# Summing three modulation sections by rows on DVE instead of TensorE, and splitting part of the weights by DMA, in an RG-LRU and retention trunk

## Chip, cores and metric

One NeuronCore of one Trainium2 chip. Times are device microseconds (us) of one execution. The kernel before was run three times; the changed kernel is compared by its median.

## What is computed

Two layers act on 512 latent tokens and 256 context tokens (768 in all) of width 1024. Cut to what matters here:

```python
def modulation(cond, mod_w, mod_b):            # cond: (1024,), mod_w: (1024, 3072)
    m = silu(cond) @ mod_w + mod_b
    return split(m, 3)                          # shift, scale, gate

def trunk_layer(x, ctx, c, c_ctx, ...):
    sh, sc, gt = modulation(c, mod_w, mod_b)
    shc, scc, gtc = modulation(c_ctx, mod_w, mod_b)
    h = rmsnorm(x, norm_g) * (1 + sc) + sh      # ctx the same way, with shc and scc
    y, yc = mixer(h, hc, need_ctx_out)
    x = x + gt * y
    if need_ctx_out:                            # layer 0 only
        ctx = ctx + gtc * yc
```

Layer 0 has the RG-LRU mixer: `u = h @ w_in` (1024 to 4096: 2048 channels of the recurrent branch and 2048 of the gate branch), a convolution over 4 tokens, two gates per direction from 128 x 128 blocks, a scan forwards and one backwards, and `(sum of scans * silu(gate branch)) @ w_out`. Layer 1 has bidirectional retention with four heads. A final RMSNorm follows. Everything is float32.

The modulation of layer 0 has the sections shift, scale and gate, 1024 columns each; shift and scale are needed before the first product. The gate of layer 0 and the shift and scale of layer 1 are needed later. These three are the sections that the change is about.

## The kernel before

**Products.** A float32 product is three float32r matmuls (`mm3`, L75 to L78): both operands are split into a rounded part hi and a rest lo, and lo\*hi, hi\*hi and hi\*lo are added up in PSUM. One product of a weight tile of 128 x 1024 with all 768 tokens is 48 matmuls of 128 x 384.

**Weights.** A table `order` (L98 to L112) lists all weight tiles in the order of their use. `load` (L80) fetches one by a DMA from SP's queue into a buffer `wraw`; `split_w` (L85) makes hi with an ACT copy (L91) and lo with a DVE subtraction (L92). The pool `wp` has four buffers each for `wraw`, `whi` and `wlo`. `take` (L144) hands out the next split tile and sees to it that the three tiles after it are split too, so entry i of the table gets its `whi` buffer when the product of entry i-4 is done.

**Layer 0.** The 2048 channels are 16 tiles c (`CT`). After the first part (norm, shift and scale, three products along with it) `iteration(c)` runs for c = 0 to 15 (L420): the product wx of the recurrent branch of tile c+2, `x_post` (convolution, ACT L260 and DVE L264), the product wg of the gate branch of tile c+1, `g_post` (SiLU: ACT L276, DVE L277), the four gate products q0 to q3 of tile c with a half-sized weight tile (ACT L452), `x_split` (hi and lo of the next tile: ACT L270, DVE L271), units of the output product (`wout_unit`, by `UNITS` one or two in most iterations from c = 4 on, none in c = 0 to 3, 7 and 11), and then the elementwise chain: exponential, tanh and square on ACT (L467 to L470), two multiplications on DVE (L471, L472), a square root on ACT (L483), the scans on DVE (L486 to L492), and y with its hi and lo (DVE L498, L499, L501; ACT L500). A unit needs y of four tiles: unit 0, in c = 4, needs those of tiles 0 to 3. Four PSUM slots are handed out in rotation.

**The three sections.** `mod_steps` (L174) works a section off in steps: per 128 rows of the matrix one load of 512 KB and two matmuls of 32 x 512 with the two condition vectors as the stationary operand (L182); at the end an ACT copy of the rows (L185), four matmuls that turn them (`mod_sum`, L172) and a DVE addition of the bias (L189). `mod_pull` is called three times in an iteration and takes `PULL[c]` steps each time, so the sections run in c = 1, 2 and 3. Meanwhile the fourth PSUM slot is theirs, and the rotation has three. In layer 1 another section is already summed by rows on DVE, with the condition broadcast to all partitions (`cb`) and a multiplication that adds up along the row (L781).

The instructions of an engine run in the order in which a list scheduler has put them; each engine works through its list without overtaking.

## Time and profile before

| | |
|---|---|
| three runs | 1081.18, 1082.06, 1083.04 us; median 1082.06 |
| profiled execution | 1082.99 us, span 1081.2 us, granted TensorE clock 0.994 |
| busy, share of the span | PE 98%, DVE 65%, ACT 53% |
| DMA | 95.56 MB, 88 GB/s in the mean |

The span runs from the first to the last instruction that the profile shows; the profiled execution's own time is 1.8 us longer. Busy shares are means over the whole span; the stage of interest is that of iterations 0 to 15 of layer 0, from about 61 to 515 us. PE is TensorE, DVE is VectorE, ACT is ScalarE, POOL is GpSimd, SP is SyncE.

### The profile page before, as it was taken

Reading aid. Unit: us, or ns where it says so; the run is one execution under the profiler, and the core shown is the slowest. Engines: PE = TensorE matmul, PEld = TensorE weight load, DVE = VectorE, ACT = ScalarE, POOL = GpSimd, SP = SyncE. Lnnn points to the kernel's source line nnn. Section 1 sums busy time; section 2 is a strip of 40 time slices with the busy share of each in tenths; the row PEclk is TensorE's granted clock in tenths of the full one; section 3 lists DMA queues with packets and bytes.
Section 4 is the critical chain, followed back from the end, with each engine's and each line's share of the span. In section 5 each row is a group of like instructions: output and inputs, shape, how many; then the busy total and the mean of one; then the engine's idle time right before and its main releaser. Section 6 shows DMA issues by size and latency. Waiting matters only on the chain.

```text
span 1081.2 us, 15148 instructions
## 1 busy us (share of the span) xinstructions
PE 1058.2 (98%) x6284; PEld 965.0 (89%) x6284; DVE 706.8 (65%) x991; ACT 573.0 (53%) x745; POOL 1.1 (0%) x5
## 2 busy tenths in 40 slices
PE   8999999999999999999999999999999999999996
PEld 7898789999999999998889988899888988889886
DVE  4777667886788777878989755462555525544256
ACT  5557778766687468788366343132432324222254
POOL 0000000000000000000000000000000000000000
PEclk9999999999999999999999999999999999999998
DMA  9524653221222121222113512311122112231102
GB/s 361 220 73 154 205 169 115 69 71 66 69 69 65 53 67 41 78 71 77 68 40 118 195 39 78 98 59 39 59 77 79 59 39 63 74 98 41 39 1 79
DMA packets 29045, 95.56 MB, mean 88 GB/s; under 512 B 2992, under 2 KB 6192, under 8 KB 27952
## 3 DMA queue, kind: packets, MB, share of 16 engines
q1 hardware_dynamic: 28976, 94.59, 26.8%
q8 instruction: 49, 0.80, 0.3%
q14 instruction: 20, 0.16, 0.0%
HBM read 92.48 MB, written 2.10 MB: 87 GB/s over the span
## 4 chain that ended last, share of the span: by engine, by line
PE 64%; ACT 7%; DVE 6%; issue 2%; DVEq 0%
PE ps L76 21%; PE ps L77 21%; PE ps L78 21%; ACT g L468 1%; ACT a L467 1%; DVE xl L264 1%; DVE g L486 1%; ACT q L470 1%; ACT L483 1%; ACT L467 1%; ACT g L452 1%; DVE q L499 1%; DVE q L492 1%; DVE q L498 1%; ACT q L483 1%
## 5 line engine op out<-in xcount | busy, mean ns | idle before, releaser
L76 PE MATMUL ps<-hl,whi 128*128 128x384 f32 (+2 forms) x816 | 286.3, 351 | 1.6 <-DVE hl L228 1.4
L78 PE MATMUL ps<-hh,wlo 128*128 128x384 f32 (+2 forms) x816 | 283.3, 347 | 0.1
L77 PE MATMUL ps<-hh,whi 128*128 128x384 f32 (+2 forms) x816 | 282.9, 347 | 0.0
L91 ACT ACTIVATE whi<-wraw 128x1024 fp32r<-128x1024 f32 (+1 forms) x125 | 125.0, 1001 | 216.9 <-PE ps L77 174.0
L92 DVE TENSOR_TENSOR wlo<-wraw,whi 128x1024 fp32r<-128x1024 f32 (+1 forms) x126 | 145.1, 1153 | 95.6 <-ACT whi L91 75.0
L76 PEld LDWEIGHTS ps<-hl,whi 128*128 128x128 f32 x816 | 153.5, 188 | 18.8 <-issue 3.5
L78 PEld LDWEIGHTS ps<-hh,wlo 128*128 128x128 f32 x816 | 153.4, 188 | 11.0 <-issue 0.8
L77 PEld LDWEIGHTS ps<-hh,whi 128*128 128x128 f32 x816 | 153.5, 188 | 10.3 <-issue 1.0
L76 PE MATMUL ps<-yl,whi 128*128 128x384 f32 (+2 forms) x416 | 143.6, 345 | 3.9 <-DVE yl L501 2.1
L78 PE MATMUL ps<-yh,wlo 128*128 128x384 f32 (+2 forms) x416 | 142.6, 343 | 0.0
L77 PE MATMUL ps<-yh,whi 128*128 128x384 f32 (+2 forms) x416 | 142.5, 343 | 0.0
L77 PE MATMUL ps<-whi,hh 128*128 128x256 f32 x384 | 108.7, 283 | 0.0
L78 PE MATMUL ps<-whi,hl 128*128 128x256 f32 x384 | 108.6, 283 | 0.0
L76 PE MATMUL ps<-wlo,hh 128*128 128x256 f32 x384 | 108.6, 283 | 0.0
L76 PEld LDWEIGHTS ps<-yl,whi 128*128 128x128 f32 x416 | 78.3, 188 | 11.7 <-DVE yl L501 2.9
L78 PEld LDWEIGHTS ps<-yh,wlo 128*128 128x128 f32 x416 | 78.3, 188 | 5.7
L77 PEld LDWEIGHTS ps<-yh,whi 128*128 128x128 f32 x416 | 78.3, 188 | 5.5
L77 PEld LDWEIGHTS ps<-whi,hh 128*128 128x128 f32 x384 | 73.7, 192 | 0.3
L76 PEld LDWEIGHTS ps<-wlo,hh 128*128 128x128 f32 x384 | 73.7, 192 | 0.3
L78 PEld LDWEIGHTS ps<-whi,hl 128*128 128x128 f32 x384 | 73.7, 192 | 0.0
L452 ACT ACTIVATE g<-ps,vt 128x768 f32<-128x768 f32 x64 | 56.2, 897 | 9.1 <-PE ps L78 8.9
L264 DVE SCALAR_TENSOR_TENSOR xl<-ps,vt,xl 128x255 f32<-128x255 f32 (+1 forms) x96 | 54.3, 605 | 0.0
(190 smaller groups left out, 1553.9 us busy)
## 6 DMA issues: line engine op xcount, KB each, us to landing
wraw<-in_ret_w_in_dram SPq DMA_DIRECT2D x48, 512.0 KB, 3.5
wraw<-in_lru_w_in_dram SPq DMA_DIRECT2D x32, 512.0 KB, 3.7
mraw<-in_lru_mod_sc_dram SPq DMA_DIRECT2D x8, 1024.0 KB, 8.8
wraw<-in_ret_mod_w_dram SPq DMA_DIRECT2D x16, 512.0 KB, 4.8
wraw<-in_lru_w_out_dram SPq DMA_DIRECT2D x16, 512.0 KB, 3.5
wraw<-in_ret_w_out_dram SPq DMA_DIRECT2D x16, 512.0 KB, 3.6
wraw<-in_lru_w_g_dram SPq DMA_DIRECT2D x16, 256.0 KB, 2.7
wraw<-in_lru_mod_gt_dram SPq DMA_DIRECT2D x8, 512.0 KB, 4.2
```

Source lines behind the costliest of these rows:

```text
L76: nc.tensor.matmul(ps, lhsT=lhs[0], rhs=rhs[1], start=first, stop=False)
L77: nc.tensor.matmul(ps, lhsT=lhs[0], rhs=rhs[0], start=False, stop=False)
L78: return nc.tensor.matmul(ps, lhsT=lhs[1], rhs=rhs[0], start=False, stop=last)
L91: nc.scalar.activation(out=hi, in_=raw, func=AF.Copy)
L92: nc.vector.tensor_tensor(out=lo, in0=raw, in1=hi.bitcast(F32), op=ALU.subtract)
L264: nc.vector.scalar_tensor_tensor(out=t[:, o0:o1], in0=u[:, o0 + sh:o1 + sh], scalar=cw[j], in1=t[:, o0:o1], op0=ALU.mult, op1=ALU.add)
L452: nc.scalar.activation(out=t, in_=ps[:, 128:896], func=AF.Sigmoid, bias=vt[:, boff:boff + 1])
L467: nc.scalar.activation(out=a, in_=r, func=AF.Exp, scale=sneg[:, d * CT + c:d * CT + c + 1])
L468: nc.scalar.activation(out=r, in_=r, func=AF.Tanh, scale=spos[:, d * CT + c:d * CT + c + 1])
L470: nc.scalar.activation(out=q, in_=a, func=AF.Square)
L483: nc.scalar.activation(out=q, in_=q, func=AF.Sqrt)
L486: nc.vector.tensor_tensor(out=i, in0=i, in1=q, op=ALU.mult)
```

## The change

The three sections no longer run on PE. Their matrices come transposed from the host, so that a row holds all 1024 inputs of one output. `cond_row` loads one condition vector, broadcast to 128 partitions, and makes its SiLU in place (sigmoid on ACT, multiplication on DVE). Per 128 outputs, one load of 512 KB and one DVE instruction with a sum along the row (L401 of the changed kernel) give the result. Both vectors are needed, so each matrix is read twice: 48 loads and 48 DVE instructions in place of 24 loads, 48 pairs of matmuls and the turning. `PULL` spreads them over iterations 0 to 12; no PSUM slot is set apart.

For the table entries that are added in iterations 1 to 12 (45 of them, 33 whole and 12 half-sized), hi is written by a DMA from POOL's queue that casts from the float32 in HBM (`cast_w`, L97), lo is begun by ACT as the negative of hi (L102) and finished by a second DMA from POOL's queue that adds the float32 values from HBM (`rest_w`, L103). ACT L91, DVE L92 and the `wraw` buffer fall away for these entries.

```diff
@@ -92,17 +92,33 @@
         nc.vector.tensor_tensor(out=lo, in0=raw, in1=hi.bitcast(F32), op=ALU.subtract)
         return hi, lo
 
+    def cast_w(src, n):
+        hi = wp.tile([P, n], F32R, tag="whi", name="whi")
+        nc.gpsimd.dma_start(out=hi, in_=src)
+        return hi
+
+    def rest_w(hi, src, n):
+        lo = wp.tile([P, n], F32R, tag="wlo", name="wlo")
+        nc.scalar.activation(out=lo, in_=hi.bitcast(F32), func=AF.Copy, scale=-1.0)
+        nc.gpsimd.dma_start(out=lo, in_=src, accum_op=ALU.add)
+        return hi, lo
+
     EARLY = (15,)
-    PULL = {1: 4, 2: 3, 3: 2}
+    PULL = {0: 1, 1: 2, 2: 2, 3: 2, 4: 1, 5: 1, 6: 1, 7: 1, 8: 1, 9: 1, 10: 1, 11: 1, 12: 1}
+    DMA_C = range(1, 13)
+    by_dma = set()
     UNITS = {4: [0], 5: [1, 2], 6: [3], 8: [4], 9: [5, 6], 10: [7], 12: [8], 13: [9], 14: [10], 15: [11]}
     order = [(lru_w_in[0, 0], 1024), (lru_w_in[0, 1], 1024), (lru_w_in[1, 0], 1024)]
     for c in range(CT):
+        n0 = len(order)
         if c + 2 < CT:
             order.append((lru_w_in[c + 2, 0], 1024))
         if c + 1 < CT:
             order.append((lru_w_in[c + 1, 1], 1024))
         order.append((lru_w_g[c], 512))
         order += [(lru_w_out[i // 4, i % 4], 1024) for i in UNITS.get(c, [])]
+        if c in DMA_C:
+            by_dma.update(range(n0, len(order)))
     order += [(lru_w_out[3, dp], 1024) for dp in range(4)]
     for h in range(HEADS):
         wq, wk = ([(ret_w_in[o + 2 * h + d], 1024) for d in range(2)] for o in (0, 8))
@@ -116,15 +132,15 @@
     def fetch_to(i):
         while len(raws) <= min(i, len(order) - 1):
             src, n = order[len(raws)]
-            raws.append((load(src, n), n))
+            raws.append(((cast_w if len(raws) in by_dma else load)(src, n), n))
 
     def split_to(i, pool=wp, dve=False):
         i = min(i, len(order) - 1)
         fetch_to(i)
         while len(ready) <= i:
-            raw, n = raws[len(ready)]
-            raws[len(ready)] = None
-            ready.append(split_w(raw, n, pool, dve))
+            j, (raw, n) = len(ready), raws[len(ready)]
+            raws[j] = None
+            ready.append(rest_w(raw, order[j][0], n) if j in by_dma else split_w(raw, n, pool, dve))
 
     def split_y(i, t, d, dve):
         fetch_to(i)
@@ -170,28 +186,6 @@
 
     def mod_sum(rows, cols, sel, w, pt):
         nc.tensor.matmul(pt, lhsT=rows[:, cols], rhs=vt[:, sel:sel + w], start=True, stop=True)
-
-    def mod_steps(rowp, boff, m, sections, banks):
-        for n, (s, src) in enumerate(sections):
-            bank = banks[n % 2]
-            for k in range(KD):
-                raw = load(src(k))
-                yield
-                for q in range(2):
-                    j = 2 * q + k % 2
-                    nc.tensor.matmul(bank[32 * j:32 * j + 32, :], lhsT=cond[:, k, :], rhs=raw[:, q * 512:(q + 1) * 512],
-                                     start=(k < 2), stop=(k >= KD - 2), tile_position=(0, 32 * j))
-            rows = rowp()
-            nc.scalar.activation(out=rows, in_=bank, func=AF.Copy)
-            for f in range(4):
-                mod_sum(rows, slice(f * P, (f + 1) * P), V_SEL, 4, bank[:, 4 * f:4 * f + 4])
-            lo = 8 * s
-            nc.vector.tensor_tensor(
-                out=m[:, lo:lo + 8, :].rearrange("p (q f) t -> p q f t", f=4),
-                in0=bank[:, 0:16].rearrange("p (f q t) -> p q f t", f=4, t=2),
-                in1=vt[:, boff + lo:boff + lo + 8].rearrange("p (q f) -> p q f", f=4).unsqueeze(3)
-                .to_broadcast([P, 2, 4, 2]), op=ALU.add)
-            yield
 
     def token_sums(ps, sq, n):
         for t in range(n // P):
@@ -386,11 +380,30 @@
         gate0 = [m0[:, 16:24, 1:2], m0[:, 16:24, 0:1]]
         rot[:] = [3, 0, 1, 2]
 
+        cr = one.tile([P, D], F32, name="cr")
+
+        def cond_row(t):
+            nc.sync.dma_start(out=cr, in_=crow[t * D:t * D + D].partition_broadcast(P))
+            for a, b in ((0, 512), (512, 1024)):
+                sg = e("sg")[:, 0:b - a]
+                nc.scalar.activation(out=sg, in_=cr[:, a:b], func=AF.Sigmoid)
+                nc.vector.tensor_tensor(out=cr[:, a:b], in0=cr[:, a:b], in1=sg, op=ALU.mult)
+
         def mods():
-            lb, rb2 = [slots[3][:, 0:512], slots[3][:, 512:1024]], [slots[3][:, 512:1024], slots[3][:, 0:512]]
-            yield from mod_steps(lambda: e("rows")[:, 0:512], V_LMB, m0, [(2, lambda k: lru_mod_gt[k * P:(k + 1) * P, :])], lb)
-            yield from mod_steps(lambda: e("rows")[:, 0:512], V_RMB, m1, [
-                (s, lambda k, s=s: ret_mod_w[k * P:(k + 1) * P, s * 1024:(s + 1) * 1024]) for s in range(2)], rb2)
+            lg, rg = (lru_mod_gt, m0, 16, V_LMB, 8), (ret_mod_w, m1, 0, V_RMB, 16)
+            row = None
+            for t, (src, m, n0, boff, nt) in ((0, lg), (1, lg), (1, rg), (0, rg)):
+                if t != row:
+                    cond_row(t)
+                    row = t
+                for f in range(nt):
+                    raw = load(src[f])
+                    nc.vector.scalar_tensor_tensor(out=raw, in0=raw, scalar=1.0, in1=cr, op0=ALU.mult, op1=ALU.mult,
+                                                   accum_out=m[:, n0 + f, t:t + 1])
+                    if f == nt - 1:
+                        o = m[:, n0:n0 + nt, t]
+                        nc.vector.tensor_tensor(out=o, in0=o, in1=vt[:, boff + n0:boff + n0 + nt], op=ALU.add)
+                    yield
             nc.vector.scalar_tensor_tensor(out=g1, in0=m1[:, 8:16, :], scalar=1.0,
                                            in1=vt[:, V_RG:V_RG + KD].unsqueeze(2).to_broadcast([P, KD, 2]),
                                            op0=ALU.add, op1=ALU.mult)
@@ -419,8 +432,6 @@
 
         def iteration(c):
             pull = PULL.get(c, 0)
-            if c == 1:
-                rot[:] = [i for i in rot if i != 3]
             if c + 2 < CT:
                 us[c + 2] = psum()
                 mm_in(take(), us[c + 2])
@@ -456,7 +467,6 @@
             mod_pull(pull)
             if c == max(PULL):
                 mod_pull(100)
-                rot.append(3)
             for i in units:
                 wout_unit(i)
             x = xl.pop(c)
@@ -770,7 +780,7 @@
 
         gate1 = one.tile([P, KD, 1], F32, name="gate1")
         cb = one.tile([P, D], F32, name="cb")
-        nc.sync.dma_start(out=cb, in_=crow.partition_broadcast(P))
+        nc.sync.dma_start(out=cb, in_=crow[0:D].partition_broadcast(P))
         nc.scalar.activation(out=cb, in_=cb, func=AF.Silu)
         gts = list(range(KD))
 
@@ -932,9 +942,9 @@
     xT = np.concatenate([g['ctx'][0], g['x'][0]], axis=0).T
     mw = g['lru_mod_w']
     msc = mw[:, 0:2048].reshape(KD, P, 2, KD, P).transpose(3, 1, 2, 0, 4).reshape(KD, P, 2048)
-    a = {'xT': xT, 'vec': _pack(g), 'trig': _trig(), 'lru_mod_sc': msc, 'lru_mod_gt': mw[:, 2048:], 'lru_w_in': win, 'lru_w_g': wg,
-         'lru_w_out': wo, 'ret_mod_w': g['ret_mod_w'][:, :2048],
-         'ret_mod_gt': g['ret_mod_w'][:, 2048:].T.reshape(KD, P, D), 'crow': g['c'].reshape(D), 'ret_w_in': rwl, 'ret_w_out': rwo}
+    a = {'xT': xT, 'vec': _pack(g), 'trig': _trig(), 'lru_mod_sc': msc, 'lru_mod_gt': mw[:, 2048:].T.reshape(KD, P, D), 'lru_w_in': win, 'lru_w_g': wg,
+         'lru_w_out': wo, 'ret_mod_w': g['ret_mod_w'][:, :2048].T.reshape(16, P, D),
+         'ret_mod_gt': g['ret_mod_w'][:, 2048:].T.reshape(KD, P, D), 'crow': np.concatenate([g['c'].reshape(D), g['c_ctx'].reshape(D)]), 'ret_w_in': rwl, 'ret_w_out': rwo}
     return {n: np.ascontiguousarray(v) for n, v in a.items()}
```

The list scheduler moves instructions. Three places, in lists of each engine; names behind an arrow are what is read, and brackets hold what the row waits for (PE, DVE, Activation, DMAHW for a DMA of SP's queue, DMASW for one of POOL's).

ACT, at the end of the first part, before:

```order
L223 ACTIVATE hh<-nx,m_81,g_82 128x256 [waits DVE_49]
L223 ACTIVATE hh<-nx,m_81,g_82 128x512
L227 ACTIVATE tmp<-nx,m_81,g_82 128x512
L91 ACTIVATE whi<-wraw 128x1024 [waits DMAHW4_49]
L332 ACTIVATE rows<-ps_70 128x128 [waits PE_49,Activation_49]
L223 ACTIVATE hh<-nx,m_81,g_82 128x256 [waits DVE_49]
L223 ACTIVATE hh<-nx,m_81,g_82 128x512
```

and in the changed kernel:

```order
L221 ACTIVATE tmp<-nx,m_81,g_82 128x512
L326 ACTIVATE rows<-ps_70 128x128 [waits PE_49,Activation_49]
L217 ACTIVATE hh<-nx,m_81,g_82 128x256 [waits DVE_49]
L217 ACTIVATE hh<-nx,m_81,g_82 128x512
L221 ACTIVATE tmp<-nx,m_81,g_82 128x512
L389 ACT_TABLE_LOAD
L389 ACTIVATE sg<-cr 128x512 [waits DMAHW7_49]
L91 ACTIVATE whi<-wraw 128x1024 [waits DMAHW4_49,PE_49]
L91 ACTIVATE whi<-wraw 128x1024 [waits DMAHW5_49,PE_49]
```

The hi of table entry 3 (the first L91 in each) stood within the loop of the first part, waiting for its load alone; now it stands behind the loop and behind the first sigmoid of `cond_row`, and waits for PE as well, since the cast of entry 6, issued at the start of the program, holds the fourth `whi` buffer.

DVE, from the backward scan of tile 1 (L490; L500 in the changed kernel) to the SiLU of the gate branch of tile 3 (L277; L271), before:

```order
L490 SCALAR_TENSOR_TENSOR q<-a,g_1110 128x256 [waits DVE_49,Activation_49]
L264 SCALAR_TENSOR_TENSOR xl<-ps_68,vt,xl 128x255 [waits DVE_49]
L492 SCALAR_TENSOR_TENSOR q<-a,q,g_1110 128x512 [waits DVE_49]
L264 SCALAR_TENSOR_TENSOR xl<-ps_68,vt,xl 128x511
L498 TENSOR_TENSOR q<-q 128x768 [waits DVE_49]
L264 SCALAR_TENSOR_TENSOR xl<-ps_68,vt,xl 128x255
L499 TENSOR_TENSOR q<-q,sil 128x768 [waits DVE_49]
L264 SCALAR_TENSOR_TENSOR xl<-ps_68,vt,xl 128x511
L92 TENSOR_TENSOR wlo<-wraw,whi 128x1024 [waits DMAHW4_49,Activation_49]
L501 TENSOR_TENSOR yl<-q,yh 128x768 [waits Activation_49]
L277 TENSOR_TENSOR sil<-ps_69,sil 128x768 [waits Activation_49]
```

and in the changed kernel:

```order
L500 SCALAR_TENSOR_TENSOR q<-a,g_1103 128x256 [waits DVE_49,Activation_49]
L401 SCALAR_TENSOR_TENSOR wraw,m_81<-wraw,cr 128x1024 [waits DMAHW5_49]
L502 SCALAR_TENSOR_TENSOR q<-a,q,g_1103 128x512 [waits DVE_49]
L401 SCALAR_TENSOR_TENSOR wraw,m_81<-wraw,cr 128x1024 [waits DMAHW6_49]
L508 TENSOR_TENSOR q<-q 128x768 [waits DVE_49]
L265 TENSOR_TENSOR xlo<-xl,xh 128x768 [waits Activation_49]
L509 TENSOR_TENSOR q<-q,sil 128x768 [waits DVE_49]
L401 SCALAR_TENSOR_TENSOR wraw,m_81<-wraw,cr 128x1024 [waits DMAHW7_49]
L511 TENSOR_TENSOR yl<-q,yh 128x768 [waits Activation_49]
L271 TENSOR_TENSOR sil<-ps_67,sil 128x768 [waits PE_49,Activation_49]
```

The subtraction L92 is gone and three of the summing instructions L401 stand between the scans and y. Between the SiLU L271 of tile 2 in one iteration and that of tile 5 three iterations later the changed list has 24 of them; eight stand ahead of that and 16 in iterations 7 to 9.

POOL and ACT, for the entries added in iteration 3; before, POOL has no row here. POOL in the changed kernel:

```order
L97 DMA whi<-in_lru_w_in_dram 128x1024 [waits DMASW4_49,PE_49]
L103 DMA wlo<-in_lru_w_in_dram 128x1024 [waits DMASW5_49,PE_49,Activation_49]
L97 DMA whi<-in_lru_w_in_dram 128x1024 [waits DMASW6_49,PE_49]
L97 DMA whi<-in_lru_w_g_dram 128x512 [waits DMASW7_49,DMASW0_49,PE_49]
L103 DMA wlo<-in_lru_w_in_dram 128x1024 [waits Activation_49]
L103 DMA wlo<-in_lru_w_g_dram 128x512 [waits DMASW1_49,PE_49,Activation_49]
L97 DMA whi<-in_lru_w_in_dram 128x1024 [waits DMASW2_49,PE_49]
```

and ACT there, from the first gates of tile 2:

```order
L463 ACTIVATE g_1291<-ps_68,vt 128x768 [waits PE_49]
L463 ACTIVATE g_1299<-ps_69,vt 128x768 [waits PE_49]
L102 ACTIVATE wlo<-whi 128x512 [waits DMASW7_49,DMASW1_49]
L463 ACTIVATE g_1307<-ps_70,vt 128x768 [waits DVE_49,PE_49]
L264 ACTIVATE xh<-xl 128x768
L510 ACTIVATE yh<-q 128x768 [waits DMAHW2_49,DVE_49]
L270 ACTIVATE sil<-ps_67 128x768
L463 ACTIVATE g_1315<-ps_67,vt 128x768 [waits DVE_49,PE_49]
L477 ACT_TABLE_LOAD
L477 ACTIVATE a<-g_1291,sneg 128x768 [waits Activation_49]
```

On POOL's one queue the half-sized cast stands ahead of the addition for the tile before it. On ACT the negative of a half-sized hi (L102) stands ahead of the gates q2 and q3 (L463), of xh (L264) and of yh (L510), and waits for its cast.

## Rows read from the trace of the kernel before

**Rows 1.** Page of the whole span: busy time by engine, the chain that ended last

```profile
PE 1058.2 (98%) x6284; PEld 965.0 (89%) x6284; DVE 706.8 (65%) x991; ACT 573.0 (53%) x745; POOL 1.1 (0%) x5
...
PE 64%; ACT 7%; DVE 6%; issue 2%; DVEq 0%
```

**Rows 2.** Windows, all engines: engine busy (instructions), TensorE clock, DMA share, GB/s

```profile
10.00:20.00 10.00, 7.05 (x56) 6.78 (x55) 7.22 (x9) 7.13 (x15) 0.00 (x0) 0.90 1.03 411
...
78.15:172.87 94.72, 93.81 (x535) 76.98 (x534) 64.45 (x79) 69.98 (x84) 0.00 (x0) 1.00 0.56 184
95.62:123.34 27.72, 27.69 (x158) 20.70 (x157) 19.76 (x25) 19.97 (x25) 0.00 (x0) 1.00 0.63 214
...
206.56:233.71 27.15, 26.21 (x150) 25.89 (x149) 22.68 (x30) 20.67 (x25) 0.00 (x0) 1.00 0.22 68
...
299.76:325.61 25.85, 24.89 (x142) 24.31 (x141) 22.57 (x29) 20.78 (x24) 0.00 (x0) 1.00 0.24 72
...
389.95:419.17 29.22, 29.22 (x170) 29.22 (x169) 20.97 (x25) 20.54 (x25) 0.00 (x0) 1.00 0.20 63
```

**Rows 3.** Line L182, and windows of L182 alone: PE busy, PEld busy

```profile
L182 PE MATMUL ps<-wraw,cond x96: 592/592/617, 91.1 to 166.6; 128*32 128x512 f32 x96
...
78.15:172.87 94.72, 17.15 (x96) 2.90 (x96) 1.00 0.56 184
```

**Rows 4.** PE timeline, iterations 0, 1 and 5: start, duration, what ran

```profile
78.50 0.34 PE L76 MATMUL ps<-xlo,whi 128*128 128x384 f32 x1
78.67 0.34 PE L77 MATMUL ps<-xh,whi 128*128 128x384 f32 x1
...
91.14 1.91 PE L182 MATMUL ps<-wraw,cond 128*32 128x512 f32 x12
...
197.69 0.34 PE L76 MATMUL ps<-hl,whi 128*128 128x384 f32 x1
```

**Rows 5.** DVE timeline: SiLU of tiles 2 and 5, lo of y, row sums

```profile
105.91 0.94 DVE L277 TENSOR_TENSOR sil<-ps,sil 128x768 f32<-128x768 f32 x1
...
189.34 0.95 DVE L501 TENSOR_TENSOR yl<-q,yh 128x768 fp32r<-128x768 f32 x1
190.21 0.95 DVE L277 TENSOR_TENSOR sil<-ps,sil 128x768 f32<-128x768 f32 x1
...
586.87 1.22 DVE L781 SCALAR_TENSOR_TENSOR wraw<-wraw,cb 128x1024 f32<-128x1024 f32 x1
588.01 0.08 DVE L781 DVE_READ_ACCUMULATOR wraw<-wraw,cb 128x1 f32 x1
```

**Rows 6.** Windows of L92 alone: DVE busy

```profile
95.62:123.34 27.72, 3.12 (x3) 1.00 0.63 214
```

**Rows 7.** ACT timeline, end of the first part: hi of entries 3 and 4

```profile
48.58 1.04 ACT L91 ACTIVATE whi<-wraw 128x1024 fp32r<-128x1024 f32 x1
...
61.01 1.06 ACT L91 ACTIVATE whi<-wraw 128x1024 fp32r<-128x1024 f32 x1 [1.96 <-PE ps L77]
```

**Rows 8.** PE timeline, products of entry 3 within the first part (first and last of seven)

```profile
58.58 0.33 PE L76 MATMUL ps<-hl,whi 128*128 128x384 f32 x1
...
59.62 0.66 PE L76 MATMUL ps<-hl,whi 128*128 128x384 f32 x2
```

**Rows 9.** DMA issues: queue, count, KB each, median us from issue to landing

```profile
wraw<-in_lru_w_in_dram SPq DMA_DIRECT2D x32, 512.0 KB, 3.7
mraw<-in_lru_mod_sc_dram SPq DMA_DIRECT2D x8, 1024.0 KB, 8.8
...
wraw<-in_lru_w_g_dram SPq DMA_DIRECT2D x16, 256.0 KB, 2.7
```

**Rows 10.** Waits of the whole span: us in total, times, longest

```profile
ACT whi L91 <- PE ps L77: 174.0, 63, 6.4
DVE wlo L92 <- ACT whi L91: 75.0, 51, 4.1
```

**Rows 11.** Groups by line, shapes apart: DVE L92, ACT L91 (busy, mean ns)

```profile
L92 DVE TENSOR_TENSOR wlo<-wraw,whi 128x1024 fp32r<-128x1024 f32 x110 | 134.1, 1220 | 87.9 <-ACT whi L91 67.4 <-PE ps L759 20.0
...
L91 ACT ACTIVATE whi<-wraw 128x1024 fp32r<-128x1024 f32 x109 | 115.1, 1056 | 195.2 <-PE ps L77 153.6 <-PE ps L78 26.4 <-issue 9.6
```

## Prediction

> **What bounds the kernel now.** Read first the page's busy line and the chain that ended last [rows 1]: PE is busy 98% of the span, DVE 65%, ACT 53%, and the chain lies on PE for 64%. So a microsecond taken off PE counts, unless another engine is late at that place. That is read next, from the windows of single iterations [rows 2]. An iteration with one unit lasts 29.22 us with PE busy throughout (389.95:419.17): PE bounds it. An iteration without a unit lasts 25.85 us (299.76:325.61) with PE 24.89, DVE 22.57 and ACT 20.78 busy; its PE work is less than the period. Consecutive matmuls of 384 columns start 0.17 us apart [rows 4]; at the 0.1735 us that the stretch there gives, a product of 48 is 8.33 us, the 24 of the gates 4.2 us, and two products and the gates 20.8 us. So without units the loop of ACT and DVE (scan chain, PSUM slots to be read out) sets some 25.85 us, where PE by itself would need 20.8.
>
> Iterations 1 to 3 have no units, but the modulation matmuls. There an iteration lasts 27.72 us with PE busy for 27.69 and DVE for 19.76 (95.62:123.34) [rows 2]: PE is full, though DVE and the loop behind it are not far from it. This is where the change works.
>
> **What it removes from PE.** 96 matmuls of 592 ns are listed on L182, but pass through in groups: 12 of them take 1.91 us [rows 3, 4], 0.16 each, and the windows put 17.15 us of PE on that line. With the turning matmuls, the stops around each group and waits for loads, the stretch from 78.15 to 172.87 us holds 94.72 us for 535 matmuls [rows 2], 414 of which are of 384 columns (the rest are the 96, 24 for the turning and one): 414 x 0.1735 = 71.8, so 22.9 us go elsewhere, of which about 22 belong to the sections and 1 to stalls. The most the removal alone can give is 22 us.
>
> **What it adds to DVE there, and why little of the 22 arrives.** Between the SiLU of tile 2 (105.91 us) and that of tile 5 (190.21) [rows 5] three iterations pass in 84.3 us. In the changed list DVE does all that it did there but L92 (3.12 us in an iteration [rows 6]), so 19.76 - 3.12 = 16.6 us, three times: 49.9. To this come 24 row sums. The kernel has the same instruction in layer 1: it starts at 586.87 and its accumulator is read at 588.01 [rows 5], a pitch of 1.14 us: 24 x 1.14 = 27.4. Two multiplications of `cond_row` are about 1.2 us (bounds 0.6 and 1.3 each pair, between a half and a whole L92 of 1.22 us [rows 11]). Together 78.5 us of DVE without a gap; I take 79.6, with a third of a microsecond of waiting in each iteration. So **DVE becomes the bound of these three iterations**, 26.5 us each, in place of PE's 28.1: 4.7 us less, not 22.
>
> **What comes earlier and takes some back.** (a) The cast of entry 6 is issued first of all, with no wait. The loads then fill the DMA engines: 411 GB/s at a share of 1.03 from 10 to 20 us [rows 2]. Another 0.52 MB delays the inputs by at most 1.3 us, and by 0 if it lands behind them; I take 1.3. (b) The hi of entry 3 was made at 48.58 us, so seven matmuls of its product ran from 58.58 to 59.62 us [rows 7, 8], while PE waited for the last tile of h; now it is made behind the loop, where that of entry 4 stands (61.01). This costs 7 x 0.17 = 1.2 us of filling, and up to 1.1 more if PE waits for the hi. I take 1.2. Eight row sums fall into iteration 0, whose DVE had gaps. The start loses 2.5 us.
>
> **What arrives on PE.** Unit 0 needs y of tile 3, the row before the SiLU of tile 5. It ends where this SiLU starts: 105.91 + 2.5 + 79.6 = 188.0, against 190.2 before. What depends on it is a quarter of the unit, 12 matmuls, 2.1 us. The rest of iteration 4 and the products before it PE has done by then, since its own work is 22 us less. So wx of tile 7 starts at 190.1 instead of 197.69 [rows 4]: **7.5 us gained.** PE had let 187 to 197.69 go by on work that it can now do ahead.
>
> **What is given back after that.** PE runs ahead of `x_post` and `g_post` now and waits for a PSUM slot in iteration 5: the iteration before it already held a stall (26.21 busy of 27.15 [rows 2]), and I take 1 us more. In iterations 7 and 11, which the ACT and DVE loop sets, 0.75 us each: the negative of the half-sized hi waits on ACT for a cast that starts only when PE gives the buffer back, and the gates q2, q3 and xh stand behind it, while ACT's copy had its data at hand. Bounds: 0, since ACT already waits up to 6.4 us at that place [rows 10], and 2.7 us each, a load of 256 KB [rows 9]. The 16 row sums of iterations 7 to 9 cost nothing: DVE has 20.97 of 29.22 us busy in an iteration with a unit, and in the others loses its L92s for them. Give-back 2.5 us; net 5.0.
>
> **What the split by DMA costs.** ACT's negative takes the place of the copy (1.06 us either way [rows 11]). The path of a weight tile becomes longer: PE gives a buffer back, POOL casts, ACT negates, POOL adds. No row shows a DMA of POOL or one that adds. Nearest are SP's loads: 2.7 us for 256 KB, 3.7 for 512, 8.8 for 1 MB [rows 9]. I take 4.5 for the cast (with the generation of its descriptors), 5.5 for the addition, which moves its destination too, 1.06 for ACT and up to 4 of waiting on ACT's list: 11 to 15 us; bounds 6.5 and 24 us. The buffer comes free three products before it is needed, 20.8 us, more with a unit. So it is hidden, and costs nothing by itself; if the cover goes, PE waits for lo. The Trainium skill ("DMA: Bandwidth & Descriptors", section "Anatomy of one DMA") prices a transfer issued by GpSimd at 2.0 us plus bytes by 436 GB/s, an estimate of 3.2 us for 512 KB, by which the path would be 3.6 us shorter and the sum the same. DMA traffic in iterations 1 to 3 rises from 184 to some 300 GB/s, below the 411 of the start.
>
> **Sum:** 1082.99 (the profiled execution, 0.9 above the median of the runs shown) - 7.5 + 2.5 = **1078.0 us**. Against the median this is 0.4% less; 0.2% is about what a measurement can tell, so faster means below 1079.9 and slower above 1084.2.
>
> **Rivals.**
> 1. *DVE's gaps absorb the row sums, PE gets all.* Then about 22 - 2.5 = 19.5 us go: 1063 to 1065. For it: DVE has 8 us idle in an iteration [rows 2]. Against: at PE's own 20.8 us an iteration DVE would have 3 x 20.8 - 49.9 = 12.5 us free, and the row sums need 27.4; units of later iterations would have to fill PE meanwhile, and they need y. Chance 0.06.
> 2. *Nothing is left.* The 7.5 us are given back wholly, to the start (up to 2.4 for entry 3), PSUM slots and the waits for casts (2.7 each in seven iterations): 1080 to 1084. Chance 0.18.
> 3. *Slower: the path through POOL is too long.* POOL's queue is one and in order; a cast that waits for PE holds up the addition of the tile before it, so a late addition delays the next cast. While cast, negative and addition stay under the three products (20.8 us without a unit, about 25 with) nothing is lost; it decides from about 25 us. At 28 us PE loses 3 us or more about every four entries, eight times in iterations 5 to 12: +24 - 7.5, about 1097; at 26 us 1083. For it: 8.8 us for a transfer that does twice the traffic [rows 9], two of them in a row, waits of 4 to 6 us on ACT [rows 10]. Against: the DMA engines are at a share of 0.20 to 0.24 there [rows 2], and medians are 3.7. Chance 0.30. A rule of the Trainium skill speaks for it ("SBUF — State Buffer", "Who interferes with whom"): DVE in a two-port mode locks GpSimd out of the port that it needs to write descriptors, and it advises against issuing from GpSimd under DVE work. By it each of POOL's DMAs could wait for one DVE instruction; no run here shows that yet.
>    The longest DVE instruction near is under 2 us, so two such delays add under 4 us to a path of 11 to 15, which stays below 20.8: by themselves they do not decide.
> 4. *The split by DMA does not take work from DVE where it counts*, because DVE waits on ACT there anyway: 75 us of DVE's idle time already lie before L92 [rows 10]. Then the three iterations keep their 28 us: this ends in case 2, and is counted there.
>
> **How the numbers follow.** Forecast 0.46 (1075 to 1079.9; 1078), case 1 0.06, case 2 0.18, case 3 0.30. Faster is forecast and case 1: 0.52; same is case 2: 0.18; slower 0.30. The range goes from 1069, about halfway from the forecast to case 1, to 1097, the 28 us path: left out are most of case 1 and the tail of case 3, under 0.2. The likeliest case's own range is 1074 to 1080.
>
> **What would show it.** In the changed profile: no L182; DVE nearly without idle time between the SiLUs of tiles 2 and 5, some 79 to 80 us apart; wx of tile 7 at about 190 us; POOL's DMAs landing in 4 to 6 us; lo of a weight ready before its product, hence few waits of PE's weight loads for L78. Wrong it is if PE waits for POOL's additions in iterations 5 to 12, if ACT's negatives wait long for casts with gates behind them, or if the three iterations last under 24 us each.

## The result, and the profile after

The changed kernel takes 1118.87 us in the median of 4 runs (1112.8 to 1121.64), the kernel before 1082.55 in 4 runs beside it: a ratio of 1.0324, 95% interval 1.0301 to 1.0348. It is 36 us slower; 1078 was forecast, within 1069 to 1097.

The page of the changed kernel, busy time by engine, then the chain that ended last (its first shares):

```profile
PE 1051.3 (94%) x6164; PEld 973.1 (87%) x6164; DVE 719.6 (64%) x1049; ACT 574.3 (51%) x748; POOL 65.7 (6%) x95
...
PE 63%; issue 18%; DVE 6%; ACT 6%; DMA 5%; POOL 2%; SPq 1%; DVEq 0%; POOLq 0%; ACTq 0%
```

Against [rows 1] PE has 120 instructions less (the 96 of L182 and the 24 for the turning), but only 6.9 us less of busy time, and the span is 36.5 us longer: PE stands idle some 43 us more. DVE, which was to be relieved of 45 subtractions and given 48 row sums, is busy 13 us longer. DMA and POOL now stand on the chain. Its 18% of "issue" name no cause: the longest pieces are stretches in which POOL stands between two of its DMAs, such as 11.03 us from 105.37, which its own row below puts down to a wait for ACT.

Where the time went is seen best from one instruction that every iteration has once: DVE's forward scan of 768 elements. Its starts in us, from the DVE timelines of one profiled execution each (experiments beside, their names are explained below; the profiled executions of e3 and e13, 1105.2 and 1090.4 us, are the fastest of their four, 5 to 6 us below their medians):

| scan of tile | before | change | e1 rows only | e3 no early cast | e4 half tiles old | e13 late half negatives | e10 rows spread |
|---|---|---|---|---|---|---|---|
| 0 | 95.6 | 109.0 | 95.4 | 97.4 | 95.3 | 96.5 | 96.9 |
| 4 | 206.6 | 226.4 | 207.3 | 214.9 | 211.5 | 215.5 | 205.4 |
| 8 | 325.6 | 352.8 | 329.5 | 341.7 | 329.5 | 333.0 | 320.0 |
| 12 | 445.0 | 481.8 | 447.8 | 467.3 | 450.8 | 453.4 | 439.5 |

Of 36.8 us at tile 12, 13.4 are lost before the first scan, 6.4 between the scans of tiles 0 and 4 (where the sections had been on PE, and a gain was forecast), 7.3 up to tile 8 and 9.6 up to tile 12.

**The start.** ACT, DVE and PE in windows of the change, columns as in [rows 2]:

```profile
10.00:20.00 10.00, 4.57 (x41) 4.38 (x40) 6.59 (x7) 7.59 (x16) 0.00 (x0) 0.95 1.04 405
20.00:30.00 10.00, 9.28 (x66) 8.40 (x66) 3.08 (x8) 2.72 (x6) 0.00 (x0) 0.53 0.88 333
```

The cast of entry 6 goes out at 1.27 us. The DMA engines then are as full as before (share 1.04), with 0.5 MB more to move among the inputs: the four loads of the latent tokens land after 9.5 us in the median instead of 7.3, and ACT's last squares begin at 17.43 us, 13.64 before. PE waits for the sums of squares with nothing to do (4.57 of 10 us busy, 7.05 in [rows 2]), and its granted clock, 0.95 in the mean of this window, falls to 0.53 in the mean of the next 10 us: nearly all of it at the lower of its two levels, 1.2 GHz. The first product starts at 32.24 us, 25.91 before: 6.3 us. PE in the change:

```profile
20.17 2.72 PE L192 MATMUL ps<-ones,ssum 128*128 128x1 f32 x12 [5.60 <-DVE ssum L303]
...
32.24 0.44 PE L76 MATMUL ps<-hl,whi 128*128 128x384 f32 x1 [1.14 <-DVE hl L222]
```

and before:

```profile
16.43 1.50 PE L198 MATMUL ps<-ones,ssum 128*128 128x1 f32 x12 [2.40 <-DVE ssum L309]
...
25.91 0.45 PE L76 MATMUL ps<-hl,whi 128*128 128x384 f32 x1 [1.13 <-DVE hl L228]
```

The same twelve matmuls take 2.72 us instead of 1.50. Of the 7 us that come on top until the first scan, the largest wait is in iteration 0: at 94.79 us ACT has waited 5.37 us for a half-sized cast, with two gates behind it.

The Trainium skill ("DMA: Bandwidth & Descriptors", "Issuing engines are not separate DMA queues") states that DMAs run on the same 16 engines and interleave, whoever started them. The trace agrees: a transfer on POOL's queue slowed those on SP's, 9.5 against 7.3 us.

**The iterations.** ACT in iteration 1 (start, duration, what ran, in brackets the idle time before it and who ended it):

```profile
110.15 0.20 ACT L495 ACTIVATE warm<-q 128x1 f32<-128x1 f32 x1
114.93 1.06 ACT L102 ACTIVATE wlo<-whi 128x1024 fp32r<-128x1024 f32 x1 [4.58 <-DMA whi<-in_lru_w_in_dram]
115.90 1.68 ACT L463 ACTIVATE g<-ps,vt 128x768 f32<-128x768 f32 x2
...
122.30 0.63 ACT L102 ACTIVATE wlo<-whi 128x512 fp32r<-128x512 f32 x1 [3.30 <-DMA whi<-in_lru_w_g_dram]
122.84 0.88 ACT L463 ACTIVATE g<-ps,vt 128x768 f32<-128x768 f32 x1
```

and PE at the same time:

```profile
109.01 0.34 PE L78 MATMUL ps<-xh,wlo 128*128 128x384 f32 x1
116.83 0.69 PE L76 MATMUL ps<-hl,whi 128*128 128x384 f32 x1 [7.49 <-ACT g L463]
117.32 0.53 PE L77 MATMUL ps<-hh,whi 128*128 128x384 f32 x1
```

This is the loss in one picture. ACT has done its work at 110.35 and waits 4.58 us for a cast. The two gates behind the negative on its list were computed by PE before 109.4 us and lie in PSUM. PE needs a slot for its next product, finds none, and stands for 7.49 us; when it goes on, its matmuls take 0.53 us instead of 0.34, at a granted clock of 0.50 from 116.8 to 120 us. The cast itself came late because POOL works its queue off in order:

```profile
103.94 0.87 POOL L103 DMA_DIRECT2D wlo<-in_lru_w_in_dram  x1 [6.69 <-ACT wlo L102]
104.50 0.87 POOL L97 DMA_DIRECT2D whi<-in_lru_w_in_dram  x1
116.41 0.89 POOL L103 DMA_DIRECT2D wlo<-in_lru_w_in_dram  x1 [11.04 <-ACT wlo L102]
```

POOL waits for ACT's negative (until 103.94), only then issues the next cast, though PE had given back the buffer by 98.9; the cast lands 10 us after its issue, the longest of the 45, and ACT's next negative waits for that. ACT and POOL wait for each other in turn. From 60 to 500 us PE stops like this, for a slot that a gate holds, for 27.7 us; the other 13.9 us are waits for `x_post`, the longest 9.1 us at 366 us, where the negative of a unit's tile had waited 7.37 us for its cast with yh behind it on ACT's list. In the whole kernel, what line L102 (the negatives on ACT) waited for, us and times:

```profile
  DMA whi<-in_lru_w_in_dram: 39.2, 16
  DMA whi<-in_lru_w_g_dram: 23.0, 6
  DMA whi<-in_lru_w_out_dram: 11.0, 3
```

and line L97 (the casts on POOL's queue), from issue to landing:

```profile
DMA to landing us min/median/max: 2.8/6.1/10.4
```

25 of the 45 negatives waited for their cast, 73 us in all. The median cast takes 6.1 us and the median addition 5.3 (3.8 to 8.6), where SP's load of a whole tile took 3.7 [rows 9]. Half-sized casts take 5.3 in the median, nearly as much as whole ones, but that is the queue and not the size. Eight of the 12 were issued within 1.5 us of another DMA of POOL's and took 4.9 to 9.0 us; the other four, issued 3 us or more after one, took 2.8 to 3.8, where whole casts with that distance took 5.4 to 8.0. The Trainium skill ("DMA: Bandwidth & Descriptors", "Anatomy of one DMA — SWDGE (gpsimd) path") would have 3.2 us for 512 KB, an estimate from its formula; the shortest cast of that size here took 4.3 us, the median of all is nearly twice the estimate, and the measurement decides.

### The profile page after: what moved, and what is told of

It reads as the page before. It is cut to its first block, busy times and chain, and to the rows that moved or that the text cites. A ratio compares the mean times of both kernels' runs of the same rounds, so it can differ in the third digit from the quotient of the medians.

```text
span 1117.7 us, 15128 instructions
## 1 busy us (share of the span) xinstructions
PE 1051.3 (94%) x6164; PEld 973.1 (87%) x6164; DVE 719.6 (64%) x1049; ACT 574.3 (51%) x748; POOL 65.7 (6%) x95
## 4 chain that ended last, share of the span: by engine, by line
PE 63%; issue 18%; DVE 6%; ACT 6%; DMA 5%; POOL 2%; SPq 1%; DVEq 0%; POOLq 0%; ACTq 0%
PE ps L76 21%; PE ps L77 20%; PE ps L78 20%; DMA whi<-in_lru_w_g_dram 2%; DMA whi<-in_lru_w_in_dram 1%; POOL wlo L103 1%; POOL whi L97 1%; DMA acc_l<-in_xT_dram 1%; ACT g L478 1%; DMA whi<-in_lru_w_out_dram 1%; ACT a L477 1%; DVE xl L258 1%; ACT g L463 1%; DVE g L496 1%; DVE q L502 1%
## 5 line engine op out<-in xcount | busy, mean ns | idle before, releaser
L78 PE MATMUL ps<-hh,wlo 128*128 128x384 f32 (+2 forms) x816 | 284.0, 348 | 0.2 <-DVE wlo L92 0.2
L91 ACT ACTIVATE whi<-wraw 128x1024 fp32r<-128x1024 f32 (+1 forms) x80 | 82.6, 1035 | 157.3 <-PE ps L77 117.4
L78 PEld LDWEIGHTS ps<-hh,wlo 128*128 128x128 f32 x816 | 154.3, 189 | 10.2 <-DVE wlo L92 0.5
L78 PE MATMUL ps<-yh,wlo 128*128 128x384 f32 (+2 forms) x416 | 144.7, 348 | 0.0
L92 DVE TENSOR_TENSOR wlo<-wraw,whi 128x1024 fp32r<-128x1024 f32 (+1 forms) x81 | 96.4, 1195 | 63.4 <-ACT whi L91 42.8
L78 PE MATMUL ps<-whi,hl 128*128 128x256 f32 x384 | 108.6, 283 | 0.0
L76 PE MATMUL ps<-wlo,hh 128*128 128x256 f32 x384 | 108.6, 283 | 0.0
L78 PEld LDWEIGHTS ps<-yh,wlo 128*128 128x128 f32 x416 | 79.7, 192 | 5.7
L102 ACT ACTIVATE wlo<-whi 128x1024 fp32r<-128x1024 f32 (+1 forms) x45 | 42.4, 942 | 80.2 <-DMA whi<-in_lru_w_in_dram 39.2
L78 PEld LDWEIGHTS ps<-whi,hl 128*128 128x128 f32 x384 | 73.7, 192 | 0.0
L463 ACT ACTIVATE g<-ps,vt 128x768 f32<-128x768 f32 x64 | 55.4, 894 | 20.8 <-PE ps L78 20.3
```

The lines of the kernel that those rows point to most:

```text
L76: nc.tensor.matmul(ps, lhsT=lhs[0], rhs=rhs[1], start=first, stop=False)
L78: return nc.tensor.matmul(ps, lhsT=lhs[1], rhs=rhs[0], start=False, stop=last)
L91: nc.scalar.activation(out=hi, in_=raw, func=AF.Copy)
L92: nc.vector.tensor_tensor(out=lo, in0=raw, in1=hi.bitcast(F32), op=ALU.subtract)
L102: nc.scalar.activation(out=lo, in_=hi.bitcast(F32), func=AF.Copy, scale=-1.0)
L463: nc.scalar.activation(out=t, in_=ps[:, 128:896], func=AF.Sigmoid, bias=vt[:, boff:boff + 1])
```

## The experiments

Two theories at first. **A:** the split by DMA is the loss, by the early cast at the start and by ACT's waits for casts with the gates behind them. **B:** the row sums make DVE the bound, and that is the loss. Line numbers are those of the changed kernel, a few lower down where an experiment adds lines; the kernel before took between 1083.1 and 1083.4 us beside all of these.

### e1: row sums only

```diff
-    DMA_C = range(1, 13)
+    DMA_C = ()
```

> Row sums on DVE as in the change, all weights split the old way (ACT copy, DVE subtraction). Theory A (the split by DMA is the loss: an early cast delays the inputs, and ACT's negatives wait for casts with the gates behind them): DVE has L92 back, about 29.3 us per iteration 1 to 3, so near the kernel before: 1079 to 1088 us. Theory B (the row sums make DVE the bound and are the loss): 1105 us or more.

Measured: 1085.59 us (1082.42 to 1087.52), ratio 1.0027 (1.0015 to 1.0039). B falls: row sums alone cost 2.5 us. Up to the scan of tile 4 the kernel is level with that before (table). Most of PE's 22 us have gone into its waits for a PSUM slot that ACT or DVE has yet to read, 5.45 us at the longest; from 60 to 500 us they are 21.8 us, 5.1 before:

```profile
PE ps L76 <- ACT g L463: 14.4, 5, 5.5
PE ps L76 <- DVE xl L258: 5.5, 5, 2.0
PE ps L76 <- DVE sil L271: 1.9, 3, 0.9
```

And the granted clock is 0.93 from 100 to 200 us, where it had been 1.00 (78 to 173 us, [rows 2]).

### e2: the split by DMA only

The kernel before, with `cast_w`, `rest_w` and `by_dma` of the change.

> Sections on PE as before, weights of tiles 1 to 12 split by DMA as in the change. Theory A: most of the loss is here, 1100 to 1125 us, with ACT waiting for casts and the first part some 6 us late. Theory B: 1080 to 1086 us.

Measured: 1107.22 us (1105.37 to 1109.09), ratio 1.0228 (1.0207 to 1.0249). The loss goes with the split, also where PE keeps the sections. Its first product starts at 29.37 us, 3.5 us late and not some 6 as expected; the granted clock is 0.75 from 20 to 30 us. ACT's last squares begin at 15.77, 2.1 us late against 3.8 in the change; why the same cast delays them less here isn't shown.

### e3: no early cast

```diff
             by_dma.update(range(n0, len(order)))
+            by_dma.discard(6)
```

> The change, but table entry 6 is split the old way, so no cast is issued at the start. Theory A: the inputs arrive as in the kernel before, the TensorE clock falls no longer than there, and 6 to 7 us come back: 1110 to 1114 us. If the late start has another cause (the transposed matrices, the broadcast condition), 1117 to 1121.

Measured: 1110.99 us (1105.16 to 1113.83), 7.9 less than the change, as A expected. The first product starts at 25.78 us again, and the window from 20 to 30 us shows the clock at 0.92 and DVE busy for 7.57 us, as before:

```profile
20.00:30.00 10.00, 8.72 (x103) 7.13 (x105) 7.57 (x18) 6.25 (x10) 0.00 (x0) 0.92 1.01 421
```

One cast of half a megabyte at the wrong moment cost 6 us, and some more behind it. The rest of the loss stays.

### e5: two of three negatives behind the gates

On top of e3, the negatives of the tiles wg and of the gate weights are put on ACT's list behind the last sigmoid of the iteration (in an iteration with a unit the table has more entries, and the two that move are other ones):

```diff
-                mm_in(take(), ps)
+                mm_in(take(late=c in range(1, 13)), ps)
...
-            wg = take()
+            wg = take(late=c in range(1, 13))
...
+            if c in range(1, 13):
+                with tc.issue_after(sg.ins):
+                    split_to(pos[0] + 2)
```

> As e3_no_early_cast, and the negatives of two of an iteration's three tiles stand on ACT's list behind the four gates, not ahead of or among them. Theory A: the gates no longer wait for casts, PE no longer waits for PSUM slots held by gates; 10 to 20 us less than e3, 1092 to 1103. Theory B (DVE is the bound): the same as e3 within 3 us. Third possibility: lo now arrives too late and PE waits for it at L78, then as slow as e3 or slower.

Measured: 1113.61 us (1112.03 to 1115.11). No gain: the third possibility. What PE waits for, from 60 to 500 us, in e5 (us in total, times, longest):

```profile
PE ps L78 <- DMA wlo<-in_lru_w_in_dram: 32.2, 6, 10.5
...
PE ps L76 <- ACT g L468: 0.6, 2, 0.3
```

and in e3:

```profile
PE ps L76 <- ACT g L464: 21.6, 6, 6.1
...
PE ps L76 <- DVE xl L259: 12.3, 4, 7.3
```

The wait for the gates is gone as meant, 21.6 us down to 0.6; in its place PE waits 32.2 us for lo, whose addition now starts too late: 21.2 us for wg of three tiles, and 10.8 in iterations with units for wx of two. So the place on ACT's list decides which wait it is, and neither of the two places tried for wg is free of one.

### e4: half-sized tiles the old way

```diff
-            by_dma.update(range(n0, len(order)))
+            by_dma.update(j for j in range(n0, len(order)) if order[j][1] == 1024 and j != 6)
```

> As e3_no_early_cast (entry 6 the old way), and the half-sized gate weights are split the old way too; the whole tiles stay with the DMAs. Theory A (ACT waits for casts; each weight's path through cast, negative and addition is longer than the three products that cover it): one path in three goes, POOL's queue and ACT's list are relieved, 1095 to 1105 us. Theory C (any cast on the list stops ACT as long, whole tiles decide): 1106 to 1113, as e3.

Measured: 1088.77 us (1085.42 to 1090.22), ratio 1.0046 (1.0028 to 1.0065): better than A expected. 12 half-sized tiles of 44 make 22 of the 28 us between e3 and the kernel before.

### e13: one negative behind the gates

As e5, but `mm_in(take(), ps)` stays, so that one negative of an iteration moves. In iterations 1 to 3, 7 and 11 that is the half-sized one; in 4 to 6 and 8 to 10, where the table has units in between, it is the negative of a whole tile. So the edit does not do only what the expectation says.

> As e3_no_early_cast, and only the negative of the half-sized gate weights moves, on ACT's list, from among the four gates to behind them; its product is two whole products away there. Theory A1 (what costs in the half-sized tiles is the place of their negative: the gates behind it wait for its cast and hold PSUM slots): near e4_half_tiles_old, 1088 to 1098 us. Theory A2 (what costs is that a half-sized tile takes nearly a whole tile's time on the path through POOL): as e3, 1105 to 1114.

Measured: 1095.79 us (1090.38 to 1101.29), ratio 1.0117 (1.0083 to 1.0152). 15 us come back with every DMA still there: the place of that one negative on ACT's list costs as much. That the half-sized ones make it isn't shown. By the table e13 gains nothing on e3 between the scans of tiles 0 and 4 (119.0 us against 117.6), where three of the five half-sized negatives moved; it gains 9.3 up to tile 8 and 5.2 up to tile 12, where the other two and five of the six whole ones moved. So A1 has its number, but not its reason.

### e6: split by DMA only in iterations 5, 6 and 9 to 12

```diff
-    DMA_C = range(1, 13)
+    DMA_C = (5, 6, 9, 10, 11, 12)
```

> Row sums as in the change; the split by DMA only for entries added in iterations 5, 6 and 9 to 12 (no cast at the start, none while there is no unit to cover it but in 11). Theory A: where a unit adds 8 us of products, the path is covered, so as e1_rows_only, 1083 to 1091 us. Theory C (every cast costs, wherever it stands): half the casts, half the loss between e1 and e3, 1095 to 1102.

Measured: 1093.73 us (1089.16 to 1094.78), between the two ranges: 8 us over e1. Units cover the path better, but not wholly; PE still stops for 5.60 us at 339 us behind a late `x_post`.

### e7: cast and subtract

hi by a cast as in e3, lo by a second load on SP's queue and DVE's subtraction.

```diff
-        nc.scalar.activation(out=lo, in_=hi.bitcast(F32), func=AF.Copy, scale=-1.0)
-        nc.gpsimd.dma_start(out=lo, in_=src, accum_op=ALU.add)
+        nc.vector.tensor_tensor(out=lo, in0=raw, in1=hi.bitcast(F32), op=ALU.subtract)
```

> hi by the casting DMA as in e3_no_early_cast, but lo as in the kernel before: the tile is loaded a second time by SP and DVE subtracts; ACT's negative and the adding DMA are gone. Theory A (the length of the path and ACT's place in it): the path falls to one cast and one subtraction, ACT waits for no cast, 1083 to 1093 us, the rest over e1_rows_only being DVE's waits for casts. Theory D (casts themselves, by their traffic or POOL's writing of descriptors, are too slow): 1100 us or more.

Measured: 1097.75 us (1092.52 to 1105.1). Neither range holds it. ACT waits for no cast and DVE now does, 20 us from 80 to 500 us, on a list as full as in e1 (busy 760.6 and 762.3 us). With no addition on POOL's queue the casts land sooner, from issue to landing:

```profile
DMA to landing us min/median/max: 3.0/4.5/7.2
...
whi<-in_lru_w_g_dram POOLq DMA_DIRECT2D x12, 256.0 KB, 4.1
```

against 6.1 in the median of the change, 5.3 for the half-sized ones. This speaks for the additions ahead of it on the queue as a part of what a cast took there; a second load on SP's queue was added here as well.

### e11: a fifth buffer for hi

On top of e4: `bufs=5` for `whi`, `bufs=3` for `wraw`, and each cast one entry earlier:

```diff
         fetch_to(i)
+        if i + 1 in by_dma:
+            fetch_to(i + 1)
```

> As e4_half_tiles_old, with five buffers for hi instead of four (three for the raw tiles instead of four, so that it fits), and each cast one table entry earlier; entry 7 the old way too. Theory A (the path of a tile is longer than its cover): ACT's waits for casts fall from 48 us to under 15 and the time to that of e1_rows_only or less, 1080 to 1087. Theory D (the traffic or POOL's work slows all, whatever the cover): 1087 to 1092, as e4.

Measured: 1094.62 us (1090.4 to 1096.34), slower than either expected. Half of A is confirmed: of ACT's 43 us of waits for casts in e4 none is left; all that line L102 still waits for is

```profile
  PE ps L78: 4.0, 4
```

But the buffer came from the raw tiles. The first scan starts at 99.75 us, 4.4 later than in e4, after a start with the granted clock at 0.77 from 20 to 30 us, and the row sums' loads are late now. From 60 to 340 us DVE waits

```profile
DVE wraw L403 <- DMA wraw<-in_ret_mod_w_dram: 17.8, 9, 3.3
```

So a longer cover does end the waits for casts. That the time would follow if no raw buffer had to be given for it wasn't shown: the memory for both wasn't there.

### e10 and e14: row sums spread, no split by DMA

```diff
-    PULL = {0: 1, 1: 2, 2: 2, 3: 2, 4: 1, 5: 1, 6: 1, 7: 1, 8: 1, 9: 1, 10: 1, 11: 1, 12: 1}
-    DMA_C = range(1, 13)
+    PULL = {0: 2, 1: 1, 2: 1, 3: 1, 4: 1, 5: 2, 6: 1, 8: 1, 9: 2, 10: 1, 12: 1, 13: 1, 14: 1}
+    DMA_C = ()
```

and e14 with `0: 3` in place of `0: 2` and none in 3.

> Row sums on DVE, no split by DMA, the sums spread over iterations 0 to 6, 8 to 10 and 12 to 14 so that the iterations 7 and 11 without a unit get few. Theory A (DVE bounds iterations 1 to 3 at 26 to 27 us with at most five sums each; PE is free of the sections): 3 to 8 us less than the kernel before, 1075 to 1080. Theory B (row sums cost wherever they stand): 1083 to 1090, as e1.

> As e10_rows_spread, with nine sums pulled in iteration 0, whose DVE had 9 us without work, and none in iteration 3. If DVE is the bound of iterations 1 to 3 (theory A), 1 to 3 us less than e10: 1075.5 to 1078.5 us. If the loop of ACT and DVE with its waits sets them at some 26 to 27 us anyway: 1078 to 1080, as e10.

e10: 1078.91 us (1078.51 to 1079.45), ratio 0.996 (0.9948 to 0.9973): faster than both kernels, by 4.4 us than the one before. The scans of tiles 0 to 4 lie 108.6 us apart, 110.9 before, and iterations 7 and 11 stay at 25.85. Here the gain arrives on PE as the prediction had it: wx of tile 7 starts at 188.35 us, 197.69 before, 190.1 forecast for the change. e14: 1089.02 us (1088.41 to 1090.84), against both expectations. Its iterations 1 to 4 are the shortest of all, 26.3, 25.8, 25.6 and 26.6 us, which is the loop of ACT and DVE without DVE's excess; but the scan of tile 0 comes 16 us later than before. Within iteration 0 the sums of the first section stand ahead of other work on DVE's list, and ACT waits behind them:

```profile
ACT xl L254 <- DVE m L405: 5.2, 1, 5.2
...
ACT xh L264 <- DVE xl L258: 3.4, 2, 2.5
ACT sg L389 <- DMA cr<-in_crow_dram: 2.8, 1, 2.8
```

These are the waits that the 16 us begin with; their sum isn't the whole of it.

## Why the prediction was wrong

**DVE's work in iterations 1 to 3: right; that it sets the time: only without the split.** A row sum takes 1.22 us as in layer 1. Between the SiLUs of tiles 2 and 5 the change gives DVE 78.4 us of work, 78.5 forecast:

```profile
119.35 0.95 DVE L271 TENSOR_TENSOR sil<-ps,sil 128x768 f32<-128x768 f32 x1
...
208.75 0.95 DVE L271 TENSOR_TENSOR sil<-ps,sil 128x768 f32<-128x768 f32 x1
```

```profile
119.35:208.75 89.40, 72.36 (x384) 70.78 (x383) 78.38 (x112) 61.56 (x73) 13.73 (x19) 0.91 0.83 239
```

But the SiLUs lie 89.4 us apart, not 79.6: DVE stands idle for 11 us, nearly all of it waiting for ACT. wx of tile 7 starts at 210.87 us, not 190.1. With L92 kept and no DMA split (e1) DVE is busy for 82.9 of 86.1 us there, and is the bound; before it was 84.3 us. That PE's 22 us would mostly not arrive held.

**"So it is hidden, and costs nothing by itself": this step failed.** The path of a tile was put at 11 to 15 us, with bounds of 6.5 and 24, against a cover of 20.8 us. The durations weren't far off: a cast of 6.1 us instead of 4.5, an addition of 5.3 instead of 5.5. In iteration 1, from the issue of a cast at 104.50 to the issue of its addition at 116.41, it was 11.9 us, and some 5 to land; with the wait on POOL's queue before the issue, from 98.9, it was 22.7 us, among the longest. PE's L78 waited for no addition in the change. What failed is the reading of cover. The three products only say when lo must be ready. The negative in the middle of the path stands on ACT's list in front of gates which have no such slack, and each microsecond by which its cast is late is a microsecond in which PSUM isn't read. The prediction named this as a sign of being wrong ("if ACT's negatives wait long for casts with gates behind them"), and it came: 73 us of waits for casts on ACT, and 27.7 us of stops on PE that a gate ended. The trace of before showed waits of up to 6.4 us at that place [rows 10], and they were taken for room; but they were waits for PE, which worked meanwhile, and not for a DMA, during which it ran out of work.

**The give-back of 2.5 us: the mechanism was right, its size and its reach were not.** "The negative of the half-sized hi waits on ACT for a cast that starts only when PE gives the buffer back, and the gates q2, q3 and xh stand behind it" was priced at 0.75 us each in iterations 7 and 11, with a bound of 2.7, a load of 256 KB on SP's queue [rows 9]. In these two the negative waited 2.14 and 3.96 us for its cast. The other 23 waits, 67 us, had no price at all: half-sized ones in other iterations, up to 6.2 us, and those of whole tiles. Moving the negative out from among the gates gave back 15 us (e13), taking the half-sized tiles off POOL's queue 22 (e4).

**The start: 1.3 us forecast for the cast (of 2.5 in all), 6.3 at the first product.** The delay of the inputs was bounded by bandwidth, 1.3 us, and came out at 3.8 at ACT's last squares. What was missed is the clock behind it: PE was out of work for 5.60 us, the granted clock stood at 0.50 from 20 to 28 us, and the twelve matmuls over the sums of squares took 2.72 us instead of 1.50. That the start can run at the lower level could have been read in the trace of before, whose window from 18 to 20 us stands at a clock of 0.50 as well.

**The rivals.** Rival 3 had the side, with 1097 us at 28 us of path (its own + 24 - 7.5 on 1082.99 gives 1099.5), and its trigger, an addition on POOL's queue that holds up the next cast, is what POOL's rows show. But it let PE wait for lo, and PE in the change waits for the gates and `x_post`; only e5 shows its form. It was priced from 25 us of path on, and the picture in iteration 1 came at 22.7 with the queue's wait, 17 without. So its chance of 0.30 had the right side for a reason that is half right. The lock of POOL by DVE, which the Trainium skill names ("SBUF — State Buffer", "Who interferes with whom"), does not show: POOL's issues took 0.54 to 0.92 us each, also under a DVE that was busy 87 of 100 us (from 100 to 200 us). No run tests it apart.

The steps put together, from kernel to kernel: 1083.1 before, 1085.6 with the row sums (e1), 1088.8 with the whole tiles by DMA (e4), 1111.0 with the half-sized ones (e3), 1118.9 with the early cast (the change). What stays open is how the 22 us of the half-sized tiles divide between the place of their negative and the room on POOL's queue, and what an addition costs apart from the casts beside it.

## What to carry to other kernels

A transfer has two covers: the time until its result is needed, and the time until the engine that touches it in between has other work queued behind it; the smaller one counts, and for a tile among urgent instructions it is nearly nothing. Before a step is moved to DMA, ask what each in-order list will hold behind the wait, and leave out the pieces that save least. Where an engine is freed by moving work to one that is nearly full, spread that work over the stages in which the receiver is idle: here that alone (e10 against e1, 6.7 us less with the same row sums) gave 4.4 of the 5 us that the whole change was to give.

## What had not been expected of the hardware

A DMA that casts on its way from HBM took 6.1 us in the median with additions on the same queue, and 4.5 without any (e7). What stood just ahead of it on POOL's queue counted for more than its size: half-sized casts took 4.9 to 9.0 us close behind another DMA, and 2.8 to 3.8 with 3 us or more between. An addition took 5.6 us for a whole tile of `w_in` and 3.9 for a half-sized one. And a wait of PE costs more than its length: after the 7.49 us stop the first matmuls took 0.53 us each instead of 0.34, and from 20 to 28 us of the changed kernel the granted clock was 0.50, so that 3.8 us of late inputs became 6.3 us of late products.
